# A planned decoder-step kernel: both parts of a weight tile in one buffer and one transfer, fewer transfers per inverse, and two planner margins moved

## The chip, the cores and the metric

The kernel is one program on one core of a Trainium2 chip. The metric is the device time of one execution in microseconds (us); the time before is the median of three timed runs, 1544.31 us (1543.3 to 1545.22). The engines are TensorE (PE, with its weight loads shown apart as PEld), VectorE (DVE), ScalarE (ACT), GpSimd (POOL) and SyncE (SP). In this kernel SP computes nothing: its queue issues every transfer.

## The reference

One layer of a hybrid decoder is run for a prompt of 1024 tokens and for 8 sample tokens with the same weights. Cut to what matters:

```python
p = x @ w_in                              # (T, 1024) @ (1024, 9360): GLA, RWKV-7 and gate columns
o_gla, S_gla = gla_chunked(q, k, v, log_a, S0)          # 4 heads; normed, times silu(g)
# RWKV-7, 16 heads of 64, token by token:
S = S * w[None, :] + (S @ -kk)[:, None] * (kk * a)[None, :] + v[:, None] * k[None, :]
y = S @ r                                 # then group norm, bonus, times silu(g)
m = sigmoid(gate_a) * (o_gla @ w_up_gla) + sigmoid(gate_b) * (o_rwkv @ w_up_rwkv)
out = layernorm(ALPHA * x + m @ w_out)
```

All is float32. The outputs are `out` for both groups and the new states.

## The kernel before

**Tiles and passes.** Tokens run along the free dimension in two passes: the first has 512 prompt tokens and the 8 samples, taken as 256 and 264 columns, the second has the other 512 prompt tokens in one piece. The projection goes block by block of 128 output columns (73 blocks of `w_in`, then 8 of `w_up_gla`, 8 of `w_up_rwkv`, and `w_out`). A block's weights are two half tiles of 128 x 512 (`j` = 0, 1), each with four 128 x 128 pieces.

**Three products for one.** Every float32 operand is split into a high part and a low part (`hi`, rounded; `lo = x - hi`), and a product is taken as hi·xh + hi·xl + lo·xh. `load_w` (from line 631) makes the weights' parts in the first pass: SP loads the raw half tile into `wraw`, ACT copies it to `whi`, DVE (seldom POOL) writes the difference to `wlo`. `keep` then stores both parts in DRAM, as `wh..` and `wl..`, 256 KB each. In the second pass the 146 half tiles are read back from there with two transfers each, with no work on ACT and DVE. There are four buffers `whi` and four `wlo`; `blocks` (from line 683) takes a half tile from the list `ws` and frees its two buffers after its last product.

**Pairs.** The 16 heads are done as 8 pairs in each pass, so there are 16 pairs. `front` makes the decay, key and value factors, with two sums over a head by matmul (`head_sums`, the products `big<-part,headsr`). Then come the grams: 32 products whose results DVE masks and writes to `gg` (an 'a' product and a second one, for 8 chunks and 2 heads). The 'a' products are unit triangular 64 x 64 blocks that must be inverted. Their 32 x 32 diagonal blocks go to a DRAM tile `LD` (4 transfers), from there in another arrangement to `wide` (`wide<-LD`, 4), a solve of 62 short DVE instructions fills `X` (`Xt<-X,wide` and `X<-X,Xt`), and the result goes through DRAM tile `XD` (4) to `XT` (4) and `Xs` (8); the off-diagonal blocks go to `Lp` (4). That is 28 transfers a pair. `back`, `turn`, `chain` and `norm` follow; `chain` has, for each of 8 chunks, three products in a row that wait for each other through ACT or DVE: `pch<-wide,gg`, `pch<-rh,XT`, `pch<-az,wide`.

**The samples.** The GLA state of the 8 samples is updated head by head in `gla_sample`: products `big<-row` 32 x 256, an ACT copy of 128 x 512 to a `row`, transposes `big<-cons,row`. The RWKV state of the samples (`rwkv_sample`) runs in the second pass on DVE and POOL, from eight loads `row<-state_rwkv`.

**What sets the order.** Nothing is ordered by hand. Every stage is a generator of operations, and `Order.run` (from line 368) lists them: at each step it takes the operation with the smallest modelled start time less a priority. `Order.start` models that time from when the operands are ready, with a hop between engines (`HOP`) and, for PE alone, a margin `SPARE` behind results of DVE, ACT and POOL. An operation that may run on two engines goes where it would end first. The program is that list: each engine executes its part strictly in it, and a transfer waits in SP's queue behind those ahead of it. A changed cost, margin or number of operations therefore moves rows everywhere.

Most instructions carry the line of one helper, L219, so the profile is read by the tiles' names.

Of the kernel before, what the change touches and what calls it, by code (L numbers as in the profile page):

```python
# [10 lines left out]
F32 = mybir.dt.float32  # L11
# [9 lines left out]
P = 128  # L21
D = 1024
# [4 lines left out]
HT = TP // 2  # L27
# [5 lines left out]
C = 64  # L33
NCH = HT // C
# [19 lines left out]
WBUF = {"whi": ([P, 512], 4), "wlo": ([P, 512], 4), "wraw": ([P, 512], 3)}  # L54
# [10 lines left out]
HOP = {"P": 0.2, "D": 0.8, "G": 0.14, "V": 0.14, "A": 0.14}  # L65
# [7 lines left out]
SPARE = 0.4  # L73
# [339 lines left out]
class Kern(Order):  # L413
# [217 lines left out]
    def load_w(self):  # L631

        H = NK // 2
        todo = [(b.src, b.c0, j, b.c.i) for b in self.plan if b.src is not None for j in range(2)]
        raws, his, los, kept = [], [], [], {}

        def keep(src, c0, j, hi, lo):
            for v, x in zip("hl", (hi, lo)):
                t = self.dr.tile([P, 512], F32, name=f"w{v}{c0}_{j}")
                kept.setdefault((c0, j), []).append(t)  # L640
                yield self.S.dma_start(t, x.bitcast(F32))

        def high():
            n = 0
            while True:
                yield lambda: len(raws) > n
                hi = yield from self.get("whi")
                yield self.A.copy(hi, raws[n][0])
                his.append(hi)
                n += 1  # L650
                if n == count:
                    return

        def low():
            for n in range(count):
                yield lambda: len(his) > n
                lo = yield from self.get("wlo")
                raw, src, c0, j, i = raws[n]
                yield self.E.tensor_sub(lo, raw, his[n].bitcast(F32))
                self.free(raw)  # L660
                if src is self.a["w_in"] and i == 0:
                    yield from keep(src, c0, j, his[n], lo)
                self.ws.append((his[n], lo))
                los.append(lo)
            self.w_done = True
        count = sum(src is not self.a["w_in"] or i == 0 for src, _, _, i in todo)
        self.spawn(high(), "w")
        self.spawn(low(), "w")
        for n, (src, c0, j, i) in enumerate(todo):
            if src is self.a["w_in"] and i:  # L670
                yield lambda: len(los) == len(raws)
                hi, lo = (yield from self.get("whi")), (yield from self.get("wlo"))
                for x, t in zip((hi, lo), kept[c0, j]):
                    yield self.S.dma_start(x.bitcast(F32), t)
                self.ws.append((hi, lo))
                continue
            raw = yield from self.get("wraw")
            op = self.S.dma_start(raw.rearrange("p (k c) -> p k c", c=P),
                                  src[j * H * P:(j + 1) * H * P, c0:c0 + P].rearrange("(k p) c -> p k c", p=P))
            yield from self.load(f"w{n}", op)  # L680
            raws.append((raw, src, c0, j, i))

    def blocks(self):
        xs = None
        for b in self.plan:
# [10 lines left out]
            w = []  # L696
            tiles = b.c.tiles
            todo = list(enumerate(tiles))
            while todo:
# [7 lines left out]
                for k in range(NK):  # L707
# [4 lines left out]
                    hi, lo = (x[:, k % 4 * P:k % 4 * P + P] for x in w[k // 4])  # L712
# [8 lines left out]
                    if fin and k % 4 == 3:  # L721
                        self.free(*w[k // 4])
# [378 lines left out]
    def front(self, c, p, st, d):  # L1101
# [4 lines left out]
        AZ, GG = (x.rearrange("p (c k h t) -> p c k h t", c=NCH, k=2, h=2) for x in (az, gg))  # L1106
# [72 lines left out]
        LD = self.dr.tile([4, NCH, 32, 32], F32, name=f"LD{c.i}{p}")  # L1179
# [10 lines left out]
        for q in range(4):  # L1190
            yield self.S.dma_start(L_[NU * q:NU * q + NU], LD.rearrange("n c s t -> (n c) (s t)"))
        Lp = (yield from self.get("Lp")).rearrange("p (y t) -> p y t", t=P)
        for n, b in enumerate(QS):
            h = n % 2
            yield self.S.dma_start(Lp[b, :, b], GG[QS[0], n // 2::2, 0, h, 32:64])
# [13 lines left out]
        for q in range(2):  # L1209
            b = slice(32 * q, 32 * q + 32)  # L1210
            for h in range(2):
                n = 2 * q + h
                yield self.S.dma_start(XT[HS[h]][b, :, h, b], XD[n * NCH:(n + 1) * NCH].rearrange("c s t -> s c t"))
        Xs = yield from self.get("Xs")
        xp = Xs[:, :2 * P].rearrange("p (q y t) -> p q y t", q=2, t=32)
# [311 lines left out]
    def split_out(self, raws, n):  # L1527
        for k in range(NK):
            yield lambda: len(raws) > 2 * k
            tag = "gg" if k < 2 else "wide" if k < 4 else None  # L1530
            yield lambda: k < 7 or self.w_done
            if tag == "wide":
# [7 lines left out]
            elif k < 7:  # L1540
                parts = [[x[:, :512] for x in (yield from self.get("part", 2))], (yield from self.get("lw", 2))]
            else:
                parts = [(yield from self.get("whi", 2)), (yield from self.get("wlo", 2))]
# [253 lines left out]
```

## Time and profile before

| what | value |
|---|---|
| median of 3 timed runs | 1544.31 us (1543.3 to 1545.22) |
| the profiled execution's own time | 1537.94 us |
| its span, first to last instruction | 1536.1 us |
| PE busy | 1492.0 us, 97% |
| PE weight loads busy | 1304.9 us, 85% |
| DVE, ACT, POOL busy | 1146.4, 866.7, 87.3 us |
| transfers, share of 16 engines | 70.7%, 328.60 MB |
| granted PE clock, mean | 0.995 |

The span is read in five stages: the first pass of projections (about 0 to 600 us), the second (600 to 1240), a short one in which the pairs end and the up projections begin (1240 to 1300), up and output projections (1300 to 1530), and the end. A busy PE is not a PE at its peak: the profile models the ends of its pipelined matmuls. In timeline rows the columns are start, duration, engine, line, operation, output tile and input tiles, count, and in brackets the idle time just before and what ended it.

### The profile page before, as it was taken

The page shows a single profiled execution, that of the slowest core. Times are in us where ns is not written, and L with a number is a line of the kernel's source. Part 1 is how long each engine was busy: PE and PEld are TensorE (multiplying, and loading weights), DVE is VectorE, ACT ScalarE, POOL GpSimd, SP SyncE. Part 2 cuts the span into 40 slices and gives each one's busy share as a digit, 9 for nine tenths or more (in the row PEclk, how much of TensorE's full clock was granted, in tenths as well). Part 3 has the DMA queues.
Part 4 walks back from the last instruction along what each step waited for, and adds up shares of the span by engine and source line. Part 5 has one row for each costly group of instructions (what it writes and reads, how often), then busy time and mean ns, then how long its engine had stood idle before and what let it go on. Part 6 is the DMA issues. An engine that isn't in the chain of part 4 may idle for free. (4 is left out here: it accounts for less than half of the span.)

```text
span 1536.1 us, 32633 instructions
## 1 busy us (share of the span) xinstructions
PE 1492.0 (97%) x11352; PEld 1304.9 (85%) x11352; DVE 1146.4 (75%) x3044; ACT 866.7 (56%) x2218; POOL 87.3 (6%) x202
## 2 busy tenths in 40 slices
PE   9999989999999999999999999999999999999998
PEld 8999979899999998788777778878777898988786
DVE  5785879788968896777776888888875774665665
ACT  5665576667666676564654565456346745654210
POOL 0010000001000000000001020100100000000000
PEclk9999999999999999999999999999999999999999
DMA  9878968798869887865677557656664779798522
GB/s 302 268 224 245 323 191 256 200 294 255 256 172 291 251 264 201 254 179 147 170 210 197 166 151 215 203 156 185 181 206 117 239 212 270 243 289 276 182 87 83
DMA packets 377056, 330.68 MB, mean 215 GB/s; under 512 B 131219, under 2 KB 262428, under 8 KB 376892
## 3 DMA queue, kind: packets, MB, share of 16 engines
q1 hardware_dynamic: 376892, 328.60, 70.7%
q8 instruction: 90, 1.47, 0.4%
q14 instruction: 74, 0.61, 0.1%
HBM read 198.35 MB, written 118.61 MB: 206 GB/s over the span
## 5 line engine op out<-in xcount | busy, mean ns | idle before, releaser
L219 PE MATMUL proj<-xh,whi 128*128 128x264 f32 (+2 forms) x1880 | 618.3, 329 | 5.9 <-ACT whi L219 2.7
L219 PE MATMUL proj<-xh,wlo 128*128 128x264 f32 (+2 forms) x1880 | 617.7, 329 | 0.3 <-DVE wlo L219 0.2
L219 PE MATMUL proj<-xl,whi 128*128 128x264 f32 (+2 forms) x1880 | 617.7, 329 | 0.0
L219 PEld LDWEIGHTS proj<-xh,whi 128*128 128x128 f32 x1880 | 355.6, 189 | 32.6 <-ACT row L219 3.1
L219 PEld LDWEIGHTS proj<-xh,wlo 128*128 128x128 f32 x1880 | 356.0, 189 | 24.2 <-DVE wlo L219 1.0
L219 PEld LDWEIGHTS proj<-xl,whi 128*128 128x128 f32 x1880 | 356.0, 189 | 23.4 <-issue 1.4
L219 DVE TENSOR_TENSOR wlo<-wraw,whi 128x512 fp32r<-128x512 f32 x207 | 142.2, 690 | 73.6 <-ACT whi L219 65.0
L219 ACT CAST whi<-wraw 128x512 fp32r<-128x512 f32 x210 | 129.9, 620 | 98.6 <-PE proj L219 23.1
L219 DVE TENSOR_TENSOR row<-row 128x256 f32<-128x256 f32 (+8 forms) x330 | 165.2, 509 | 20.1 <-DMA row<-state_rwkv 6.7
L219 ACT ACTIVATE row<-row 128x512 f32<-128x512 f32 (+3 forms) x229 | 138.1, 610 | 19.2 <-DVE row L219 11.2
L219 DVE TENSOR_TENSOR Xt<-X,wide 128x60 f32<-128x60 f32 (+24 forms) x496 | 105.8, 213 | 26.4 <-DMA wide<-LD 14.1
L219 DVE TENSOR_TENSOR X<-X,Xt 128x60 f32<-128x60 f32 (+24 forms) x496 | 104.7, 211 | 12.2
L219 ACT COPY rh<-pch 128x128 f32<-128x128 f32 x116 | 30.9, 267 | 131.1 <-PE pch L219 130.6
L219 ACT ACTIVATE row<-proj,omu 128x256 f32<-128x256 f32 (+1 forms) x99 | 54.1, 548 | 69.6 <-PE proj L219 68.4
L219 PE MATMUL big<-row 128*128 128x128 f32 (+4 forms) x466 | 87.0, 323 | 5.9 <-DVE row L219 4.2
L219 ACT ACTIVATE s0p<-wide,pc 64x64 f32<-64x64 f32 x256 | 89.0, 347 | 1.9
L219 POOL TENSOR_TENSOR row<-row 128x256 f32<-128x256 f32 (+7 forms) x55 | 49.5, 904 | 573.4 <-DVE row L219 313.2
L219 DVE SCALAR_TENSOR_TENSOR wide<-pch,pc,s0p 64x64 f32<-64x64 f32 x224 | 63.0, 281 | 22.8 <-PE pch L219 18.8
L219 DVE SCALAR_TENSOR_TENSOR row<-proj,pv,row 128x255 f32<-128x255 f32 (+1 forms) x99 | 56.3, 569 | 24.7 <-ACT tail L219 14.8
L219 PEld LDWEIGHTS big<-row 128*128 128x128 f32 (+3 forms) x466 | 59.0, 179 | 17.5 <-ACT row L219 6.2
L219 ACT COPY row<-big 128x128 f32<-128x128 f32 (+5 forms) x146 | 42.8, 316 | 44.9 <-PE big L219 43.9
L392 ACT ACT_TABLE_LOAD x52 | 66.7, 1283 | 0.9
(282 smaller groups left out, 2472.9 us busy)
## 6 DMA issues: line engine op xcount, KB each, us to landing
wraw<-w_in SPq DMA_DIRECT2D x146, 256.0 KB
wh<-whi SPq DMA_DIRECT2D x146, 256.0 KB
wl<-wlo SPq DMA_DIRECT2D x146, 256.0 KB
whi<-wh SPq DMA_DIRECT2D x146, 256.0 KB
wlo<-wl SPq DMA_DIRECT2D x146, 256.0 KB
wide<-LD SPq DMA_DIRECT2D x64, 128.0 KB
wraw<-w_up_gla SPq DMA_DIRECT2D x32, 256.0 KB
wraw<-w_up_rwkv SPq DMA_DIRECT2D x32, 256.0 KB
```

Source lines behind the costliest of these rows:

```text
L219: ways.append((eng, lambda call=call: call(out, *args, **kw), price(eng, name, out, args, ins)))
L392: self.nc.scalar.preload_act_table_set(self.table)
```

## The change

Three edits are made.

1. **One buffer for both parts.** `whi` and `wlo` (four of 128 x 512 each) become `wb`, four of 128 x 1024: the high part in columns 0 to 511, the low part behind it. `keep` stores a half tile with one transfer of 512 KB, rows of 4 KB, where two of 256 KB with rows of 2 KB were, and the second pass reads it back with one. `split_out` takes two `wb` for the last piece of `w_out`.
2. **The 'a' products lie together.** `gg` is laid out product by product (`k c h t`) and no longer chunk by chunk (`c k h t`), so the 16 'a' blocks of a pair are one run of 16 x 64 columns, numbered chunk by chunk with the heads inside. `LD` takes two transfers in place of four, with the same bytes; `Xs` takes four in place of eight. A pair has 22 transfers.
3. **Two margins.** `SPARE` goes from 0.4 to 0.42 and the hop from DVE from 0.14 to 0.15.

```diff
-WBUF = {"whi": ([P, 512], 4), "wlo": ([P, 512], 4), "wraw": ([P, 512], 3)}
+WBUF = {"wb": ([P, 1024], 4), "wraw": ([P, 512], 3)}
...
-HOP = {"P": 0.2, "D": 0.8, "G": 0.14, "V": 0.14, "A": 0.14}
+HOP = {"P": 0.2, "D": 0.8, "G": 0.14, "V": 0.15, "A": 0.14}
...
-SPARE = 0.4
+SPARE = 0.42
...
-        def keep(src, c0, j, hi, lo):
-            for v, x in zip("hl", (hi, lo)):
-                t = self.dr.tile([P, 512], F32, name=f"w{v}{c0}_{j}")
-                kept.setdefault((c0, j), []).append(t)
-                yield self.S.dma_start(t, x.bitcast(F32))
+        def keep(src, c0, j, x):
+            kept[c0, j] = self.dr.tile([P, 1024], F32, name=f"w{c0}_{j}")
+            yield self.S.dma_start(kept[c0, j], x.bitcast(F32))
...
-                hi = yield from self.get("whi")
-                yield self.A.copy(hi, raws[n][0])
-                his.append(hi)
+                x = yield from self.get("wb")
+                yield self.A.copy(x[:, :512], raws[n][0])
+                his.append(x)
...
-                lo = yield from self.get("wlo")
+                x = his[n]
...
-                yield self.E.tensor_sub(lo, raw, his[n].bitcast(F32))
+                yield self.E.tensor_sub(x[:, 512:], raw, x[:, :512].bitcast(F32))
...
-                hi, lo = (yield from self.get("whi")), (yield from self.get("wlo"))
-                for x, t in zip((hi, lo), kept[c0, j]):
-                    yield self.S.dma_start(x.bitcast(F32), t)
-                self.ws.append((hi, lo))
+                x = yield from self.get("wb")
+                yield self.S.dma_start(x.bitcast(F32), kept[c0, j])
+                self.ws.append(x)
...
-        AZ, GG = (x.rearrange("p (c k h t) -> p c k h t", c=NCH, k=2, h=2) for x in (az, gg))
+        AZ = az.rearrange("p (c k h t) -> p c k h t", c=NCH, k=2, h=2)
+        GG = gg.rearrange("p (k c h t) -> p c k h t", c=NCH, k=2, h=2)
+        GU = gg[:, :2 * HT].rearrange("p (u t) -> p u t", t=C)
...
-            for h in range(2):
-                yield self.S.dma_start(LD[2 * q + h].rearrange("c s t -> s c t"), GG[b, :, 0, h, b])
+            yield self.S.dma_start(LD[q].rearrange("u s t -> s u t"), GU[b, :, b])
...
-            yield self.S.dma_start(Lp[b, :, b], GG[QS[0], n // 2::2, 0, h, 32:64])
+            yield self.S.dma_start(Lp[b, :, b], GU[QS[0], n::4, 32:64])
...
-            for q in range(2):
-                u = (2 * q + n % 2) * NCH + n // 2
-                yield self.S.dma_start(xp[b, q], XD[u:(2 * q + n % 2 + 1) * NCH:2].rearrange("c s t -> s c t"))
+            yield self.S.dma_start(xp[b], XD.rearrange("(m n) s t -> n s m t", n=4)[n])
```

The list that the planner writes is new from the first rows on. PE has the same products as before; the split of copies between ACT, DVE and POOL moves by a few instructions each (DVE makes 207 of the weights' 210 low parts before and 206 now, POOL 3 and 4). SP has 1754 transfers before and 1366 now. Three places show how rows stand.

The first is PE in the first pass, at the samples of GLA head 0: the last four state products (`big<-row 32x256`) and the four transposes of their result (`big<-cons,row`), which need an ACT copy of it. Before:

```order
L219 MATMUL proj<-xl_313,whi 128x264
L219 MATMUL proj<-xh_301,wlo 128x264
L219 MATMUL big<-part,headsr 128x512
L219 MATMUL big<-row 32x256 x4
L219 MATMUL big<-cons,row 128x128 x4
L219 MATMUL proj<-xh_187,whi 128x256
```

Now, at the same head:

```order
L219 MATMUL big<-row 32x256 x4
L219 MATMUL pch<-wide,gg 128x128
L219 MATMUL proj<-xh_222,wb 128x264
L219 MATMUL proj<-xh_237,wb 128x264
L219 MATMUL proj<-xl_244,wb 128x264
L219 MATMUL proj<-xh_237,wb 128x264
L219 MATMUL proj<-xh_243,wb 128x264
L219 MATMUL proj<-xl_269,wb 128x264
L219 MATMUL proj<-xh_243,wb 128x264
L219 MATMUL big<-cons,row 128x128 x4
```

Eight products stand between the two where none stood.

The second is DVE in the second pass, at the first operation of the RWKV sample state (it reads a loaded state: `row_12160` before, `row_11648` now) and the end of a pair's `front` (up to the low half of `part`, which PE's head sum reads). The names carry buffer numbers here. Before:

```order
L219 TENSOR_TENSOR az0_167<-row_12165,row_12169 128x8x64
L219 TENSOR_TENSOR row_12161<-row_12160,row_11642 128x512
L219 SCALAR_TENSOR_TENSOR row_12167<-row_12167,row_12165 128x512
L219 TENSOR_TENSOR row_11978<-row_11978,row_12168 128x512
L219 TENSOR_TENSOR az0_167<-row_11895,row_12169 128x8x64
L219 COPY pc_12323<-row_12169 128x8
L219 COPY pc_12323<-row_12169 64x8
L219 TENSOR_TENSOR wide_12121<-row_12167,row_12166 128x8x64
L219 TENSOR_TENSOR wide_12121<-row_11978,row_12166 128x8x64
L219 SCALAR_TENSOR_TENSOR row_12168<-row_11895,pv_76,row_11978 128x512
L219 CAST part_12344<-row_12168 128x512
L219 TENSOR_TENSOR part_12345<-row_12168,part_12344 128x512
```

Now:

```order
L219 TENSOR_TENSOR wide_11546<-row_11467,row_11560 128x8x64
L219 SCALAR_TENSOR_TENSOR row_11562<-row_11340,pv_76,row_11467 128x512
L219 CAST part_11747<-row_11562 128x512
L219 TENSOR_TENSOR part_11748<-row_11562,part_11747 128x512
L219 TENSOR_TENSOR row_11643<-row_11643,row_11671 128x512
L219 TENSOR_TENSOR row_11649<-row_11648,row_11137 128x512
L219 TENSOR_TENSOR row_11467<-big_11760,row_11530 128x512
```

The state's first operation, ten rows ahead of the low half of `part` before, stands two rows behind it now.

The third is SP where the last pair's inverse ends and the up projections run: between two loads of `w_up_gla`. Before:

```order
L219 DMA wraw<-w_up_gla 128x4x128
L219 DMA mg_127<-row 128x520
L219 DMA XT_170<-XD_17660 32x8x32 x4
L219 DMA Xs<-XD_17660 32x4x32 x8
L219 DMA row<-o_rwkv 128x520
L219 DMA mg_128<-row 128x520
L219 DMA row<-o_rwkv 128x520 x7
L219 DMA az_168<-az_168 64x8x64
L219 DMA wraw<-w_up_gla 128x4x128
```

Now:

```order
L219 DMA wraw<-w_up_gla 128x4x128
L219 DMA XT_170<-XD_16831 32x8x32 x4
L219 DMA Xs<-XD_16831 32x8x32 x4
L219 DMA az_168<-az_168 64x8x64
L219 DMA row<-sg_98 128x520
L219 DMA row<-o_rwkv 128x520
L219 DMA mg_128<-row 128x520
L219 DMA row<-o_rwkv 128x520 x7
L219 DMA gg<-az_168 64x8x64 x2
L219 DMA wraw<-w_up_gla 128x4x128
```

Four `Xs` rows are gone from between the two loads, the `sg` and the two `gg` transfers have come in, and one more load of `w_up_gla` stands ahead of the group than before (15 of 16 where 14 stood).

More of the change, by code (lines that the diff above doesn't have):

```diff
@@ L656, in low @@
                 yield lambda: len(his) > n
-                lo = yield from self.get("wlo")
+                x = his[n]
                 raw, src, c0, j, i = raws[n]
-                yield self.E.tensor_sub(lo, raw, his[n].bitcast(F32))
+                yield self.E.tensor_sub(x[:, 512:], raw, x[:, :512].bitcast(F32))
                 self.free(raw)
                 if src is self.a["w_in"] and i == 0:
-                    yield from keep(src, c0, j, his[n], lo)
-                self.ws.append((his[n], lo))
-                los.append(lo)
+                    yield from keep(src, c0, j, x)
+                self.ws.append(x)
+                los.append(x)
             self.w_done = True
@@ L671, in load_w @@
                 yield lambda: len(los) == len(raws)
-                hi, lo = (yield from self.get("whi")), (yield from self.get("wlo"))
-                for x, t in zip((hi, lo), kept[c0, j]):
-                    yield self.S.dma_start(x.bitcast(F32), t)
-                self.ws.append((hi, lo))
+                x = yield from self.get("wb")
+                yield self.S.dma_start(x.bitcast(F32), kept[c0, j])
+                self.ws.append(x)
                 continue
@@ L711, in blocks @@
                         w.append(self.ws.pop(0))
-                    hi, lo = (x[:, k % 4 * P:k % 4 * P + P] for x in w[k // 4])
+                    hi, lo = (w[k // 4][:, x + k % 4 * P:x + k % 4 * P + P] for x in (0, 512))
                     xh, xl = xs[k]
@@ L721, in blocks @@
                     if fin and k % 4 == 3:
-                        self.free(*w[k // 4])
+                        self.free(w[k // 4])
                 for tt, t0, n, ps, q in qs:
@@ L1178, in front @@
         NU = 4 * NCH
-        LD = self.dr.tile([4, NCH, 32, 32], F32, name=f"LD{c.i}{p}")
+        LD = self.dr.tile([2, 2 * NCH, 32, 32], F32, name=f"LD{c.i}{p}")
         for q in range(2):
             b = slice(32 * q, 32 * q + 32)
-            for h in range(2):
-                yield self.S.dma_start(LD[2 * q + h].rearrange("c s t -> s c t"), GG[b, :, 0, h, b])
+            yield self.S.dma_start(LD[q].rearrange("u s t -> s u t"), GU[b, :, b])
         L = L_.rearrange("p (s t) -> p s t", t=32)
@@ L1211, in front @@
             for h in range(2):
[L1212 to L1213 removed]
+                yield self.S.dma_start(XT[HS[h]][b, :, h, b], XD.rearrange("(q c h) s t -> q h s c t", q=2, h=2)[q, h])
         Xs = yield from self.get("Xs")
[L1215 removed]
+        xp = Xs[:, :2 * P].rearrange("p (m t) -> p m t", t=32)
         for n, b in enumerate(QS):
[L1217 to L1219 removed]
+            yield self.S.dma_start(xp[b], XD.rearrange("(m n) s t -> n s m t", n=4)[n])
         d.AZ, d.BK, d.G, d.XT, d.v, d.bonus, d.pc, d.L = AZ, BK, GG, XT, st[2], st[1], pc, L_
@@ L1529, in split_out @@
             yield lambda: len(raws) > 2 * k
-            tag = "gg" if k < 2 else "wide" if k < 4 else None
+            tag = "gg" if k < 2 else "wide" if k < 4 else "wb" if k == 7 else None
             yield lambda: k < 7 or self.w_done
-            if tag == "wide":
+            if tag and k > 1:
                 parts = [[x[:, 0:512], x[:, 512:D]] for x in (yield from self.get(tag, 2))]
@@ L1539, in split_out @@
                 parts = [x[:2], x[2:]]
-            elif k < 7:
+            else:
                 parts = [[x[:, :512] for x in (yield from self.get("part", 2))], (yield from self.get("lw", 2))]
-            else:
-                parts = [(yield from self.get("whi", 2)), (yield from self.get("wlo", 2))]
             for hf in range(2):
```

3 lines of the change are left out of this document (1 added, 2 removed).

## The prediction

> **What bounds the kernel now.** I read the page's engine lines first, then busy time by stage, then the waits of PE, and then the timeline at PE's longest waits. The page:
>
> ```profile
> span 1536.1 us, 32633 instructions
> PE 1492.0 (97%) x11352; PEld 1304.9 (85%) x11352; DVE 1146.4 (75%) x3044; ACT 866.7 (56%) x2218; POOL 87.3 (6%) x202
> ```
>
> Busy time in the five stages, PE alone (columns: stretch, its length, PE busy with its count, granted clock, share of the DMA engines, GB/s):
>
> ```profile
> 0.00:600.00 600.00, 584.67 (x5384) 0.99 0.82 251
> 600.00:1240.00 640.00, 624.43 (x4298) 1.00 0.64 186
> 1240.00:1300.00 60.00, 54.24 (x451) 0.97 0.82 241
> 1300.00:1530.00 230.00, 228.63 (x1226) 1.00 0.61 198
> 1530.00:1536.10 6.10, 0.00 (x0) 0.77 0.25 87
> ```
>
> PE bounds every stage but the last 6 us. It idles 1536.1 - 1492.0 = 44.1 us: 15.3, 15.6, 5.8, 1.4 and 6.1 us by stage. PE's products are the same in number before and after, so the change can only win or lose idle time, and time at a lower clock. The same view of four short stretches holds much of both:
>
> ```profile
> 196.00:211.00 15.00, 9.52 (x92) 0.77 0.76 200
> 806.00:822.00 16.00, 12.50 (x107) 0.89 0.74 187
> 1245.00:1262.00 17.00, 14.48 (x106) 0.90 0.78 219
> 1270.00:1285.00 15.00, 12.12 (x99) 1.00 1.00 277
> ```
>
> Idle there: 5.48 + 3.50 + 2.52 + 2.88 = 14.4 us, a third of all in 63 us. Three of the four also show a lower clock, worth at most 0.23 x 15 + 0.11 x 16 + 0.10 x 17 = 6.9 us; where PE waits in the slow time nothing is lost, so I count 5.3 us (2.3, 1.5, 1.5).
>
> **The transfers that go.** Issue rows of SP:
>
> ```profile
> 906.04 0.32 SPq L219 DMA_DIRECT2D whi<-wh  x1
> 202.49 0.53 SPq L219 DMA_DIRECT2D wl<-wlo  x1
> 203.61 0.49 SPq L219 DMA_DIRECT2D wh<-whi  x1
> 1219.38 1.85 SPq L219 DMA_DIRECT2D LD<-gg  x4
> 1260.69 4.88 SPq L219 DMA_DIRECT2D Xs<-XD  x8
> ```
>
> Saved issue time: 146 x 0.32 us of reloads, 146 x 0.49 us of stores, 32 x 1.85/4 of `LD` and 64 x 4.88/8 of `Xs`, 47 + 72 + 15 + 39 = 173 us of SP's queue. Nearly all is hidden: the queue waits for others anyway, most of all for PE to give a weight buffer back, and PE hardly ever waits for a transfer itself.
>
> ```profile
> SPq L219 <- PE proj L219: 156.2, 103, 4.7
> PE big L219 <- DMA S<-GS: 2.0, 1, 2.0
> PE pch L219 <- DMA wide<-Sd: 1.1, 1, 1.1
> PE pch L219 <- DMA az<-wide: 1.0, 2, 0.7
> PE big L219 <- DVE Xs L219: 0.2, 1, 0.2
> ```
>
> (Columns: us in total, times, longest.) Direct waits of PE for transfers are 4.1 us and its wait for the transposed `Xs` is 0.2 us, so an inverse that ends 4 x 0.61 + 2 x 0.46 = 3.4 us earlier in each of 16 pairs gains PE 0 to 4.3 us; I take 0, since projection products cover it. Without that cover it would be up to 16 x 3.4 = 54 us.
>
> The joined reload costs nothing if it lands in time. Rows of the chain of waits:
>
> ```profile
> 1079.15 3.14 DMA whi<-wh
> 912.50 5.45 DMA wide<-LD
> 1354.10 11.10 PE pY L219 x48
> 1296.63 2.45 PE proj L219 x20
> ```
>
> A 512-wide product takes 11.10/48 = 0.231 us, a half tile 12 of them, 2.78 us. Three half tiles in hand cover 8.3 us; a transfer with 2 KB rows lands in 3.14 us, one with 4 KB rows (`wide<-LD`, 32 rows of them) in 5.45. The joined one lies between and under 8.3, so 0. If the cover were gone, the 2.3 us between the two would show at each of 146 reloads. The first pass's stores are the first rival. The grams' write to `gg` keeps 512 elements in runs of 64, so I leave its time as it is.
>
> **The four waits.** What remains is where the new list puts things. First, 203 us:
>
> ```profile
> 196.88 1.28 ACT L392 ACT_TABLE_LOAD   x1
> 202.43 0.58 ACT L219 COPY row<-big 128x512 f32<-128x512 f32 x1
> 203.07 1.12 PE L219 MATMUL big<-cons,row 128*128 128x128 f32 x4 [4.23 <-ACT row L219]
> 205.43 0.58 PE L219 MATMUL proj<-xh,whi 128*128 128x256 f32 x1 [1.24 <-ACT row L219]
> ```
>
> The transposes stand right behind the state products, and the copy that they need stands on ACT behind a table load and seven more instructions. Now eight products stand between, about 7 x 0.12 + 0.22 = 1.1 us, and ACT's list has only short chain copies and weight casts ahead of that copy. Loss now 4.23 + 1.24 + 2.3 = 7.8 us; I leave 0.5: **-7.3**.
>
> Second, 817 us:
>
> ```profile
> 791.88 5.29 SPq L219 DMA_DIRECT2D Xs<-XD  x8
> 803.97 0.48 SPq L219 DMA_DIRECT2D row<-state_rwkv  x1
> 810.44 0.69 DVE L219 TENSOR_TENSOR row<-row 128x512 f32<-128x512 f32 x1 [3.63 <-DMA row<-state_rwkv]
> 816.87 0.77 PE L219 MATMUL big<-part,headsr 128*128 128x512 f32 x1 [2.39 <-DVE part L219]
> ```
>
> DVE waits 3.63 us for the sample state, which SP issues behind the eight `Xs`, and everything that leads to `part` queues behind that; PE waits 2.39 us. Now that operation stands behind `part`, so the wait no longer reaches it: 2.39 + 1.5 of clock, **-3.9**. Late next are the operations behind it, an evacuation and the masks of the grams.
>
> Third, 1254 us:
>
> ```profile
> 1230.68 0.19 DVE L219 TENSOR_TENSOR Xt<-X,wide 128x31 f32<-128x31 f32 x1 [0.23 <-DMA wide<-LD]
> 1253.17 0.68 DVE L219 TENSOR_TENSOR part<-row,part 128x512 fp32r<-128x512 f32 x1
> 1253.91 0.80 PE L219 MATMUL big<-part,headsr 128*128 128x512 f32 x1 [2.52 <-DVE part L219]
> ```
>
> A shift on DVE, in the groups of instructions (count, busy time, mean ns of one, idle before):
>
> ```profile
> L219 DVE SCALAR_TENSOR_TENSOR row<-proj,pv,row 128x511 f32<-128x511 f32 x33 | 24.6, 745 | 7.8 <-ACT tail L219 7.3
> ```
>
> `part` stands on DVE behind the whole solve of the last pair. Between the last gram and this head sum PE's list now has 19 more products of 512, 5 more of 256 or 264 and 2 more of the chain: 19 x 0.231 + 5 x 0.12 + 2 x 0.22 = 5.4 us more. DVE's list from the last mask to `part` gains one such shift, its edge, a product and an evacuation, none of these three longer than the `part` row, and loses a small copy: at most 0.75 + 3 x 0.68 = 2.8 us. 5.4 - 2.8 = 2.6 exceeds 2.52, so the wait goes with its 1.5 us of clock: **-4.0**.
>
> Fourth, 1278 us:
>
> ```profile
> 1271.38 0.60 SPq L219 DMA_DIRECT2D wraw<-w_up_gla  x1
> 1277.45 0.62 ACT L219 CAST whi<-wraw 128x512 fp32r<-128x512 f32 x1 [13.01 <-DMA wraw<-w_up_gla]
> 1278.12 0.38 PE L219 MATMUL proj<-xh,whi 128*128 128x256 f32 x1 [2.65 <-ACT whi L219]
> ```
>
> PE ran out of weights because a load queued behind `XT`, `Xs` and eight `row<-o_rwkv`. Four issues leave (2.4 us) and one more half tile is loaded ahead, but three other transfers enter, and the DMA engines were full (share 1.00). Of 2.88 us I take half: **-1.4** (0 to -2.9).
>
> **What the list adds.** At two places `pch<-az,wide` now follows `pch<-rh,XT` with only one projection product between, about 0.23 us, where at least 0.79 us stood before. Each costs from 0 to the largest wait of such a product above, 1.1 us: **+2.0**. New long waits that I cannot see: from 0 to as much as the four that go (14.4 + 5.3 = 19.7 us), since the same planner made them. I take a quarter, nearer to 0 because the covers of head sums and chain products that I compared are otherwise alike: **+5**. The other 44.1 - 14.4 - 6.1 = 23.6 us of idle time I leave.
>
> Sum: -7.3 - 3.9 - 4.0 - 1.4 + 2.0 + 5 = **-9.6 us**. The profiled execution's own time is 1537.94 us, 1.84 above its span, and would become 1528.3. The median of the timed runs is 1544.31, 6.4 above the profiled one, so I predict **1534.7 us**.
>
> The clock terms come from the rows: waits of 2.39 and 2.52 us were each followed by a stretch at less than the full clock. The Trainium skill, "TensorE: Matmul & The Clock Gate", section "Why this matters for your kernels", asks for no idle gaps of PE over about 3 us. By that rule only the first wait would cost clock, and the sum would be 3.0 us smaller, -6.6, still within the forecast's range. The trace decides here, and it differs from the rule: shorter waits sufficed.
>
> **Rivals.**
>
> *The waits come back elsewhere* (no change). For it: all rows moved, and the four long waits are what this planner's margins let through once already. Against it: each of the four had a cause that I could find, and PE's covers did not shrink in general. With 16.6 us regained and as much lost anew: 1544 (1539 to 1549).
>
> *The stores with 4 KB rows fill the DMA engines* (slower). The place is the first pass. Its DMA share is 0.82 at 251 GB/s over 600 us, 150.6 MB, of which the stores are 146 x 0.524 = 76.5 MB, so 0.42 of share. From 43% more time per stored byte the share is 1 and the weight loads behind them set the pace; each further 10% is 0.042 x 600 = 25 us. At 50% more: 17 us, so 1534.7 + 17 = 1552. For it: `wide<-LD`, the only row with 4 KB rows, lands 128 KB in 5.45 us, where 256 KB take 3.14. Against it: it writes only 32 partitions, the stores read 128.
>
> *Nothing new goes wrong* (the whole gain). The four waits go and no long one comes: -17, 1527.
>
> That the change does not do what it says is out: the list has 32 `LD`, 64 `Xs` and 292 weight transfers where 64, 128 and 584 were.
>
> **How the numbers follow.** The forecast gets 0.54 (its own range 1527 to 1540), the waits elsewhere 0.27, the whole gain 0.11, the stores 0.08. A measurement of this kernel tells about 0.2% from no change, 3.1 us: faster is under 1541.2, slower over 1547.4. Faster: 0.54 + 0.11 + 0.05 of the second case = 0.70; same 0.15, all of the second case; slower 0.07 of the second case + 0.08 = 0.15. The range: -19 us (all waits gone, the fourth whole, 1525) to +4 (the second case's upper part, 1548); the far ends of the second case and the stores are left out.
>
> **What would show it.** In the changed profile: PE idle of some 38 us in place of 44; no wait above 2 us at the transposes of the first GLA head, nor at a head sum in front of the sample states, nor at the last pair's; full clock in the first 600 us. PE's direct waits for transfers stay near 4 us. Wrong would be: a DMA share near 1 in the first 600 us; waits of ACT for weight buffers that a store still holds; new PE waits over 2.4 us with a lower clock behind them, or waits over 1 us at `pch<-az,wide` in many chunks.

## The result and the profile after

The changed kernel takes **1535.8 us** (median of 5 runs, 1531.6 to 1537.2), the kernel before 1543.75 in the same comparison (median of 5, 1540.6 to 1545.2): ratio 0.9944, 95% interval 0.9923 to 0.9964. The forecast was 1534.7. The time came out near the forecast; the experiments below show that the sum behind it did not.

The profiled execution of the changed kernel took 1536.23 us, close to its median. That of the kernel before took 1537.94, some 6 below its own, so the two profiles differ less than the medians do. Span and PE line of the page, then PE by stage (columns as in the prediction):

```profile
span 1534.5 us, 31929 instructions
PE 1493.6 (97%) x11352; PEld 1305.9 (85%) x11352; DVE 1150.6 (75%) x3065; ACT 865.8 (56%) x2210; POOL 84.2 (5%) x189
```

```profile
0.00:600.00 600.00, 585.80 (x5433) 1.00 0.80 250
600.00:1240.00 640.00, 622.04 (x4215) 0.99 0.64 186
1240.00:1300.00 60.00, 59.11 (x506) 1.00 0.88 260
1300.00:1530.00 230.00, 226.62 (x1205) 1.00 0.61 199
```

PE idles 1534.5 - 1493.6 = 40.9 us, 3.2 less than before. Its busy time is 1.6 us more with the same 11352 products: that is time at a lower clock. The third stage gained most (54.24 to 59.11 of 60), the second pass lost (624.43 to 622.04 of 640). The same view of the four stretches of the prediction, and of three where the changed kernel loses:

```profile
196.00:211.00 15.00, 14.79 (x187) 1.00 0.87 256
806.00:822.00 16.00, 16.00 (x132) 1.00 0.62 172
1245.00:1262.00 17.00, 16.53 (x134) 1.00 0.85 265
1270.00:1285.00 15.00, 15.00 (x147) 1.00 1.07 318
845.00:862.00 17.00, 14.81 (x121) 0.90 0.49 112
1012.00:1030.00 18.00, 16.16 (x158) 0.81 0.52 143
1165.00:1182.00 17.00, 14.58 (x96) 0.80 0.58 148
```

In the first four PE is busy 62.3 of 63 us, where it was 48.6, all at the full clock. In the other three it idles 2.19 + 1.84 + 2.42 = 6.45 us, and the clock takes up to 0.10 x 17 + 0.19 x 18 + 0.20 x 17 = 8.5 us. The last of the three is not wholly new: before, PE waited 2.0 us for the same load at that head, but at the full clock. The waits of PE (us in total, times, longest):

```profile
PE big L219 <- DVE row L219: 6.3, 6, 2.0
PE big L219 <- DMA S<-GS: 4.3, 2, 2.4
PE pch L219 <- DVE az L219: 1.2, 2, 0.7
PE pch L219 <- DMA az<-wide: 1.0, 1, 1.0
```

`S<-GS` is the load of a GLA head's state, stored by the first pass; the second pass needs it once for each of four heads. It holds two of the three new stretches; the larger sum, for `row`, is spread over six waits.

### The profile page after: what moved, and what is told of

Its sections match the earlier page's. It is cut to its first block, busy times and chain, and to the rows that moved or that the text cites. A ratio compares the mean times of both kernels' runs of the same rounds, so it can differ in the third digit from the quotient of the medians.

```text
span 1534.5 us, 31929 instructions
## 1 busy us (share of the span) xinstructions
PE 1493.6 (97%) x11352; PEld 1305.9 (85%) x11352; DVE 1150.6 (75%) x3065; ACT 865.8 (56%) x2210; POOL 84.2 (5%) x189
## 5 line engine op out<-in xcount | busy, mean ns | idle before, releaser
L219 PE MATMUL proj<-xh,wb 128*128 128x256 f32 (+2 forms) x3744 | 915.6, 327 | 2.1 <-DVE wb L219 0.9
L219 PEld LDWEIGHTS proj<-xh,wb 128*128 128x128 f32 x3744 | 627.0, 189 | 49.0 <-issue 2.5
L219 PE MATMUL proj<-xl,wb 128*128 128x264 f32 (+2 forms) x1872 | 613.2, 328 | 0.0
L219 PEld LDWEIGHTS proj<-xl,wb 128*128 128x128 f32 x1872 | 354.4, 189 | 23.5 <-issue 2.1
L219 DVE TENSOR_TENSOR wb<-wraw,wb 128x512 fp32r<-128x512 f32 x206 | 141.6, 691 | 55.3 <-ACT wb L219 52.2
L219 DVE TENSOR_TENSOR row<-row 128x512 f32<-128x512 f32 (+9 forms) x342 | 167.3, 495 | 14.1 <-ACT row L219 4.9
L219 ACT CAST wb<-wraw 128x512 fp32r<-128x512 f32 x210 | 129.8, 620 | 78.4 <-PE proj L219 31.6
L219 ACT ACTIVATE row<-row 128x512 f32<-128x512 f32 (+4 forms) x229 | 138.2, 611 | 31.7 <-DVE row L219 19.8
L219 PE MATMUL big<-xh,wb 128*128 128x512 f32 (+2 forms) x272 | 70.8, 332 | 0.0
L219 PE MATMUL pY<-xh,wb 128*128 128x264 f32 (+2 forms) x256 | 63.5, 319 | 0.0
```

The lines of the kernel that those rows point to most:

```text
L219: ways.append((eng, lambda call=call: call(out, *args, **kw), price(eng, name, out, args, ins)))
```

## The experiments

Each median is over 4 to 12 runs, taken in turns with runs of the kernel before, whose median was 1542.8 to 1543.4 us in all four sets (the changed kernel's are those above, beside 1543.75). "Transfers" is how many SP issues by the trace (1752 and 1364, two fewer than were counted in the two lists); idle is span less PE's busy time of the profiled execution. That execution is one run only: it was the slowest of its kernel's runs in the tenth to the twelfth, and the fastest in the seventh.

| kernel | list of the engines | transfers on SP | median us (range) | ratio to before, interval | PE idle | PE busy |
|---|---|---|---|---|---|---|
| before | its own | 1752 | 1543 | 1 | 44.1 | 1492.0 |
| changed | its own | 1364 | 1535.8 (1531.6 to 1537.2) | 0.9944, 0.9923 to 0.9964 | 40.9 | 1493.6 |
| 1 all in two | changed | 1752 | 1562.5 (1561.2 to 1565.4) | 1.0129, 1.0114 to 1.0145 | 59.5 | 1501.0 |
| 2 margins only | new | 1752 | 1566.9 (1565.4 to 1569.5) | 1.0157, 1.0142 to 1.0173 | 60.0 | 1505.7 |
| 3 old margins | new | 1364 | 1558.4 (1558.0 to 1561.1) | 1.0104, 1.0089 to 1.0119 | 59.6 | 1496.6 |
| 4 state early | changed | 1364 | 1526.0 (1524.2 to 1526.3) | 0.9886, 0.9870 to 0.9903 | 38.8 | 1485.4 |
| 5 inverse in two | changed | 1460 | 1557.5 (1555.0 to 1558.7) | 1.0094, 1.0075 to 1.0114 | 54.7 | 1502.0 |
| 6 weights in two | changed | 1656 | 1539.6 (1532.2 to 1548.8) | 0.9986, 0.9966 to 1.0006 | 41.0 | 1494.2 |
| 7 all in two, state early | changed | 1752 | 1548.5 (1543.1 to 1552.6) | 1.0036, 1.0023 to 1.0049 | 48.5 | 1492.7 |
| 8 22 a pair | before | 1656 | 1531.0 (1529.9 to 1531.7) | 0.9924, 0.9906 to 0.9942 | 38.4 | 1489.7 |
| 9 gathers in two | changed | 1428 | 1552.6 (1549.9 to 1554.6) | 1.0065, 1.0045 to 1.0084 | 51.3 | 1500.1 |
| 10 second halves by POOL | changed | 1364 | 1538.8 (1533.6 to 1541.4) | 0.9969, 0.9952 to 0.9986 | 47.1 | 1492.5 |
| 11 state early, XT by POOL | changed | 1300 | 1522.75 (1521.8 to 1528.8) | 0.9878, 0.9857 to 0.9900 | 37.7 | 1489.3 |
| 12 as 11 | before | 1592 | 1527.0 (1526.6 to 1530.9) | 0.9895, 0.9873 to 0.9916 | 36.7 | 1492.4 |

A list is kept by leaving what the planner sees unchanged and replacing only what it emits at a place (`ways` holds what an operation issues). PE's products then stand in the same order in both kernels, and the difference of their ends, product by product, shows where time is lost.

### 1. The same list with all its transfers back

The prediction put the saved transfers at nothing. The plainest test is to give them back and leave all else.

```diff
-            yield self.S.dma_start(kept[c0, j], x.bitcast(F32))
+            op = self.S.dma_start(kept[c0, j], x.bitcast(F32))
+            t = kept[c0, j]
+            fn = lambda: [self.nc.sync.dma_start(t[:, s], x.bitcast(F32)[:, s]) for s in (slice(0, 512), slice(512, 1024))]
+            op.ways = [(op.ways[0][0], fn, op.ways[0][2])]
+            yield op
```

The reload, `LD` and `Xs` are split in the same way.

> The changed kernel's list on TensorE, VectorE, ScalarE and GpSimd, instruction for instruction, but every joined transfer (store and reload of the split weights, the inverse's read of the 32-wide blocks, the gather of its rows) is issued as two again: SyncE issues 1752 transfers as the kernel before does, not 1364. Theory A (the saved transfers are hidden; the time goes by the waits of TensorE that the list happens to hold): 1536 us, within 3, as the changed kernel's 1535.8. Theory B (the gain is the saved transfers): 1543.8, as before. Theory C (the two margins do it): 1536.

It takes 1562.5 us, 26.7 more than the changed kernel: theory A has fallen. PE by pass, and its waits for the load:

```profile
0.00:600.00 600.00, 583.77 (x5403) 1.00 0.81 248
600.00:1240.00 640.00, 607.16 (x4061) 0.98 0.61 179
```

```profile
PE big L219 <- DMA S<-GS: 12.9, 3, 5.7
```

Most is lost in the second pass. In the profiled executions the 26.3 us grow by 4.8 up to 640 us, then by some 4 at 870, 4.9 at 978, 4.4 at 1020, 3.3 at 1172 and 3.2 between 1250 and 1265 us of the changed kernel. At 870, 1020 and 1172 the wait is for `S<-GS`. SP's timeline ahead of the last of them, the changed kernel first, then this one:

```profile
1156.79 3.21 SPq L219 DMA_DIRECT2D XD<-X  x4
...
1161.56 1.82 SPq L219 DMA_DIRECT2D XT<-XD  x4
1163.42 2.12 SPq L219 DMA_DIRECT2D Xs<-XD  x4
1165.59 0.64 SPq L219 DMA_DIRECT2D az<-az  x1
1166.33 0.57 SPq L219 DMA_DIRECT2D wb<-w  x1
1166.94 0.43 SPq L219 DMA_DIRECT2D S<-GS  x1
```

```profile
1176.51 3.44 SPq L219 DMA_DIRECT2D XD<-X  x4
...
1181.98 2.15 SPq L219 DMA_DIRECT2D XT<-XD  x4
1184.17 3.77 SPq L1226 DMA_DIRECT2D Xs<-XD  x8
1187.99 0.65 SPq L219 DMA_DIRECT2D az<-az  x1
1189.05 0.83 SPq L676 DMA_DIRECT2D wb<-w  x2
1189.92 0.43 SPq L219 DMA_DIRECT2D S<-GS  x1
```

SP has no pause here. It issues one transfer after the other, about half a microsecond each (3.77 us for eight, 2.12 for four), and the state's load stands at the end of the line: 10.15 us behind the first `XD` in the one, 13.41 in the other. PE's products behind that load, in the same two kernels (in brackets the wait):

```profile
1171.84 0.79 PE L219 MATMUL big<-row,S 128*128 128x128 f32 x2 [2.42 <-DMA S<-GS]
```

```profile
1194.87 0.80 PE L219 MATMUL big<-row,S 128*128 128x128 f32 x2 [5.72 <-DMA S<-GS]
```

3.26 us later in the line, 3.30 us more of waiting. This is theory D of the later experiments: what counts is how long SP issues ahead of a load that PE, or work for PE, waits for.

### 2 and 3. The margins alone, and the rest alone

```diff
-HOP = {"P": 0.2, "D": 0.8, "G": 0.14, "V": 0.14, "A": 0.14}
+HOP = {"P": 0.2, "D": 0.8, "G": 0.14, "V": 0.15, "A": 0.14}
...
-SPARE = 0.4
+SPARE = 0.42
```

The second kernel is the one before with this edit; the third is the changed kernel with its opposite.

> The kernel before with the two margins alone (0.42 and 0.15); all transfers as before. Theory A: a new list with new waits, so anywhere from 1528 to 1548 us; the difference to 1543.8 should be found again as PE's idle time and as stretches at a clock of 0.5. Theory B: 1543.8, no difference. Theory C: 1535.8, the whole gain.

> The changed kernel's joined weights and 22 transfers a pair, with the old margins (0.4 and 0.14). Theory A: again a list of its own, 1528 to 1548 us, with idle time and stretches at 0.5 that account for it. Theory B: 1535.8, the whole gain. Theory C: 1543.8, none of it.

1566.9 and 1558.4 us: both outside every theory's range. Each part of the change alone makes the kernel slower, by 24 and 15 us. The same two margins, which change nothing but what the planner lists in which order and on which engine, cost 24 us in the kernel before and gain 23 (1558.4 to 1535.8) with the rest of the change. PE in the first pass and the longest single wait of the second kernel, then the same of the third:

```profile
0.00:600.00 600.00, 576.12 (x5240) 0.98 0.81 246
```

```profile
PE proj L219 <- ACT whi L219: 5.3, 2, 4.5
```

```profile
0.00:600.00 600.00, 576.97 (x5289) 0.99 0.80 250
```

```profile
PE big L219 <- DVE Xs L219: 4.2, 2, 3.6
```

Both lose some 8 us in a first pass that was busy 584.67 us before; besides, the one runs out of weights for 4.5 us at 1305 us, and the other waits 3.6 for an inverse's rows at 593 us, where the kernel before waited 0.2 for such rows in all. So a new list is worth some 24 us either way, several times the +5 that the prediction took for unseen waits and more than its bound of 19.7, and the time of a part alone tells nothing of that part.

### 4. The state's load at the start of the head

The load is issued where the head begins, 35 to 42 us before its use; the planner still believes it at the old place.

```diff
+        S0 = None
+        if c.i:
+            S0 = self.take("S")
+            self.nc.sync.dma_start(S0, self.GS[h])
...
-            S = yield from self.get("S")
-            yield S_.dma_start(S, self.GS[h])
+            S = S0
+            op = S_.dma_start(S, self.GS[h])
+            op.ways = [(op.ways[0][0], lambda: None, op.ways[0][2])]
+            yield op
```

> The changed kernel with one thing moved: the load of a GLA head's stored state in the second pass is issued at the start of the head and not just ahead of its use; every other instruction keeps its place on its engine. In the changed kernel TensorE waits 2.0 us at 1020 and 2.9 us at 1172 for that load, and the clock is at 0.5 for 6.83 us behind each. If these waits cost what the trace shows (about 2.4 us each of idle time and up to 3.4 us each by the clock), the time falls by 4.5 (the waits alone) to 11 us (with the clock), to 1525 to 1531 us, most likely 1527. If something else is as late there (VectorE's rows, the next bank), it falls by less than 2 us.

1526.0 us, 9.8 less than the changed kernel and 1.0 off the expectation. The last head's load, then PE in the three bad stretches (each shifted by the time gained):

```profile
1126.91 0.42 SPq L787 DMA_DIRECT2D S<-GS  x1
```

```profile
845.00:862.00 17.00, 14.81 (x129) 1.00 0.50 122
1008.00:1026.00 18.00, 17.89 (x186) 1.00 0.64 166
1154.00:1172.00 18.00, 17.62 (x134) 1.00 0.67 174
```

The two waits are gone, and the clock is full. Product by product, PE gains 5.0 us at the one place and 5.6 at the other. PE's waits there were 1.84 and 2.42 us (not the 2.0 and 2.9 of the expectation), so more than half of what each cost was clock. The smaller steps elsewhere nearly cancel: of the 10.3 us between the spans, 2.1 are idle time and 8.2 are PE's busy time, for the same products. The first stretch, which lies ahead of that head's use of the load (868 us), idles as long as in the changed kernel (2.19 us) and yet keeps the clock, so that gain, about 1.5 us, is not shown to be the load's.

### 5, 6 and 9. Which transfers

> The changed kernel's list, with the inverse's transfers alone issued in two (28 a pair, 1460 in all); the weights stay joined. Theory A has fallen by the first run (1562.5 us where it gave 1536). Theory D in its place: in the second pass SyncE issues its transfers in one line, and the load of the stored GLA state, for which TensorE waits, stands behind the inverse's gathers and one to four reloads of weights; twice the gathers keep it back by 1.65 to 2.3 us (3.77 against 2.12, 5.09 against 2.75 us), the reloads by 0.3 to 0.5 each. D gives the inverse's 96 transfers some half of the 26.6 us: 1549 us, from 1544 to 1556. Theory E (each of the 388 transfers costs alike, 0.069 us): 96 x 0.069 = 6.6, so 1542.4.

> The changed kernel's list, with the weights' stores and reloads alone issued in two (1656 transfers); the inverse has 22 a pair. Theory D: 1546 us, from 1540 to 1553 (what stands ahead of the state's load grows by 0.3 to 1.5 us, and the stretch at 989 us, where three reloads take 8.99 for 4.10 us, is theirs). Theory E: 292 x 0.069 = 20.1, so 1556.

The inverse's 96 transfers cost 21.7 us, more than theory D's range allowed, the weights' 292 cost 3.8, just under its range; the sixth kernel's interval overlaps the changed kernel's, and its 12 runs spread over 16.6 us. (The 8.99 against 4.10 us in its expectation sets three reloads beside two.) Theory E, the same price for each transfer, had 6.6 and 20.1 and falls. What matters is where a transfer stands. Of the 96, 64 are the gathers into `Xs`:

> The changed kernel's list, with only the gather of the inverse's rows into Xs issued in two (64 transfers more, 1428 in all); the read of the blocks and the weights stay joined. The fifth run put 21.7 of the 26.6 us on the inverse's 96. Theory D (what counts is how long SyncE issues ahead of transfers that TensorE or the inverse waits for): the gathers are the part that stands ahead of the state's load, so two thirds or more of 21.7: 1551 us, from 1546 to 1558. Theory E (alike for each): 64 / 96 x 21.7 = 14.5, so 1550. If the read of the blocks, which begins the inverse, counts most: 1543 or less.

1552.6 us, 16.8 more than the changed kernel for these 64. That the reading of the blocks counts most would have given 1543 or less and is out; that each of the 96 costs alike gives 1550, which this run does not tell from theory D.

### 10. The same transfers, half of the gathers issued by POOL

If SP's issue time is what counts, the second halves should cost nothing when another engine issues them.

```diff
-            yield self.S.dma_start(xp[b], XD.rearrange("(m n) s t -> n s m t", n=4)[n])
+            op = self.S.dma_start(xp[b], XD.rearrange("(m n) s t -> n s m t", n=4)[n])
+            fn = lambda n=n, b=b: [e.dma_start(xp[b, m], XD.rearrange("(m n) s t -> n s m t", n=4)[n][:, m])
+                                   for m, e in ((slice(0, 4), self.nc.sync), (slice(4, 8), self.nc.gpsimd))]
+            op.ways = [(op.ways[0][0], fn, op.ways[0][2])]
+            yield op
```

> As the ninth, with each second half of those gathers issued by GpSimd's queue, so that SyncE issues 1364 transfers as in the changed kernel, while the same 1428 transfers run. Theory D (SyncE's issue time is what counts): back to the changed kernel's 1536 us, within 4. Theory G (smaller transfers land later or fill the DMA engines): as the ninth run, 1546 to 1558. If GpSimd's issue is slow (no row shows one), between the two, with TensorE waiting for Xs.

1538.8 us: 13.8 of the 16.8 are back, with the same 1428 transfers. The other 3.0 are within the runs' ranges; in its profile, a slow one, PE still waits 6.5 us for the state's load (8.5 in the ninth, 4.3 in the changed kernel). Timelines at the third head, SP of the ninth kernel, then SP of the tenth and its POOL:

```profile
1019.24 5.11 SPq L1214 DMA_DIRECT2D Xs<-XD  x8
1024.39 0.66 SPq L219 DMA_DIRECT2D az<-az  x1
```

```profile
1009.73 2.81 SPq L1214 DMA_DIRECT2D Xs<-XD  x4
1012.58 1.51 SPq L219 DMA_DIRECT2D az<-az  x1
```

```profile
1008.09 1.66 POOL L1214 DMA_DIRECT2D Xs<-XD  x3 [5.78 <-PE big L219]
```

Theory G, that smaller transfers land later or fill the DMA engines, would have left it where the ninth is. Theory D stands: it is SP's time to issue them. The Trainium skill, "DMA: Bandwidth & Descriptors", section "Rules for kernel authors", says that spreading transfers over issuing engines adds no bandwidth and saves only the sequencer's issue time; the run agrees with the saving, which was the 13.8 us here, and tests nothing of the bandwidth.

### 7. All transfers in two, the state's load early

> The first experiment's kernel (the changed list, all transfers in two, 1752) with the state's load moved to the start of the head, as in the fourth. Theory D, if the state's load is the one transfer that matters: its three waits (12.9 us) go, and with them most of what the clock took (PE's busy time is 7.4 us above that of the changed kernel): 1562.5 - 20 = 1542 us, and between 1536 and 1546. If the saved transfers count at many places, it stays at 1550 or above.

1548.5 us, 14 below the first kernel but 22.5 above the fourth: between the two cases of the expectation. So the state's load is not the only one that the line holds back, and, of what the split costs, not the main part: with that load out of the way the split transfers still cost 22.5 us, against 26.7 with it in its old place. Product by product against the fourth kernel (17.3 us between the two profiles, as the seventh's was its fastest run) it loses 7.7 us up to 640 us in steps of 1 to 2 us, and 4.5 at once at 987 us, where a load of an RWKV state is late:

```profile
PE pch L219 <- DMA wide<-Sd: 4.6, 2, 3.6
```

### 8. The old list with 22 transfers a pair

The changed layout of `gg` and the joined reading and gathering, in the kernel before with its own list; the weights stay in two, the margins are the old ones. The planner still counts 28: it sees both halves, the first issues the whole and the second nothing.

```diff
-            yield self.S.dma_start(xp[b], XD.rearrange("(m n) s t -> n s m t", n=4)[n])
+            for m in (slice(0, 4), slice(4, 8)):
+                op = self.S.dma_start(xp[b, m], XD.rearrange("(m n) s t -> n s m t", n=4)[n][:, m])
+                fn = (lambda: None) if m.start else lambda n=n, b=b: self.nc.sync.dma_start(
+                    xp[b], XD.rearrange("(m n) s t -> n s m t", n=4)[n])
+                op.ways = [(op.ways[0][0], fn, op.ways[0][2])]
+                yield op
```

> The kernel before with its own list on TensorE, VectorE, ScalarE and GpSimd, and only the inverse's transfers joined (22 a pair, 1656 in all), which its planner did not know of. Theory D: that list holds one wait for the state's load (2.0 us at 1170, behind 6.80 us from issue to use), so 1 to 4 us are to be had: 1541 us, from 1538 to 1544. Theory E: 96 x 0.069 = 6.6, so 1536.7. Theory A: 1543.

1531.0 us, 11.8 less than before and 4.9 less than the changed kernel: more than any theory gave. SP at the last head, the kernel before and then this one:

```profile
1156.45 3.78 SPq L219 DMA_DIRECT2D Xs<-XD  x8
...
1165.88 0.45 SPq L219 DMA_DIRECT2D S<-GS  x1
```

```profile
1151.40 1.92 SPq L1223 DMA_DIRECT2D Xs<-XD  x4
...
1160.22 0.42 SPq L219 DMA_DIRECT2D S<-GS  x1
```

PE of this kernel in the prediction's first three stretches (the third shifted by 7 us) and at that head:

```profile
196.00:211.00 15.00, 9.52 (x86) 0.66 0.74 194
806.00:822.00 16.00, 13.99 (x111) 0.89 0.47 139
1160.00:1182.00 22.00, 21.61 (x207) 1.00 0.35 85
1238.00:1256.00 18.00, 15.33 (x111) 0.91 0.78 225
```

At the head PE was busy 19.62 of the same 22 us before. The first and the third long wait are still there (4.23 and 2.67 us), as they must be if the list makes them; the second is shorter (12.50 busy before), because the sample state behind the gathers comes sooner (DVE waits 1.68 us for it, 3.63 before). The fourth, for weights whose load stood behind the gathers, falls from 2.65 to 0.73 us, with no change of the list.

### 11 and 12. SP's line made shorter still

The four gathers into `XT` go to POOL's queue, on top of the state's early load; first in the changed kernel, then in the eighth.

```diff
-                yield self.S.dma_start(XT[HS[h]][b, :, h, b], XD.rearrange("(q c h) s t -> q h s c t", q=2, h=2)[q, h])
+                op = self.S.dma_start(XT[HS[h]][b, :, h, b], XD.rearrange("(q c h) s t -> q h s c t", q=2, h=2)[q, h])
+                fn = lambda q=q, h=h, b=b: self.nc.gpsimd.dma_start(
+                    XT[HS[h]][b, :, h, b], XD.rearrange("(q c h) s t -> q h s c t", q=2, h=2)[q, h])
+                op.ways = [(op.ways[0][0], fn, op.ways[0][2])]
+                yield op
```

> The fourth kernel (state's load at the start of the head, 1526 us) with the four gathers into XT, which stand ahead of the four into Xs and take SyncE 1.8 to 2.2 us a pair, issued by GpSimd's queue. Theory D: Xs and all behind it come 2 us earlier in 16 pairs; what PE still waits for there (0.9 us for Xs, 1.1 us for a state of the other layer) is small with 22 transfers, so 0 to 4 us: 1523 us, from 1520 to 1526. If GpSimd issues much slower than SyncE, XT is late at the products that follow and the time rises to 1530 to 1540.

> The eighth kernel (the list of before, weights in two, 22 transfers a pair, 1531 us) with the two moves of the eleventh: the state's load at the start of the head, the gathers into XT on GpSimd's queue. If the lists are worth the same once SyncE's line is short, it comes to the eleventh's 1523 us, within 3. If the list of before has nothing that waits behind SyncE any more (its trace shows no wait for the state's load), it stays at 1531, from 1528 to 1533, and the new list with its joined weights is the better one by 8.

1522.75 and 1527.0 us. The eleventh is the fastest kernel here, 13 us below the changed one, and as expected; its interval overlaps the fourth's, so the step from 1526.0 to 1522.75 is not told from nothing. The twelfth lies between the two cases of its expectation. The two differ by 4.3 us, within the runs' ranges; and since the twelfth also has its weights in two, which cost 3.8 in the sixth, this says nothing of the lists.

## Why the prediction was right, and where it was not

**The time was right by luck: two wrong terms cancelled.** The prediction had -9.6: nothing for the transfers (but for a part of the fourth wait), the rest for the list. The runs have a gain from the transfers and a loss from the list, by either road: the old list with 22 transfers a pair is 11.8 us faster, and the rest of the change then costs 4.9; or the new list with all transfers costs 19 us, and joining them gains 26.7. Each list was made for its own number of transfers, so neither road gives the one true share of each. Nor can the terms be settled one by one: they were read from the profiled execution, and between the two profiled executions the change is 1.6 us, where the forecast had 9.6; only the medians differ by 7.95.

**"Nearly all is hidden"** is the step that failed. It took SP's 173 us as hidden since SP mostly waits for PE, and bounded the gain of the inverse by PE's direct waits for transfers, 4.1 us in all (4.4 with `row<-OS`, which it left out). The runs give 26.7 us for all 388 transfers and 21.7 for the inverse's 96. Both averages look away from the place that matters. SP waits long on the whole, but not between an inverse's first `XD` and what follows it: there the issue time is the path (10.15 against 13.41 us). And the direct waits are those of a list that was made with 28 transfers; they don't bound what stands just inside its cover, nor what goes through another engine. The prediction's own rows for 817 us show such a case, DVE waiting 3.63 us for a sample state issued behind eight `Xs`; I read it as a matter of DVE's order alone.

**The joined weights, 0,** are not contradicted: taking them apart costs 3.8 us, with overlapping intervals. PE's wait for the state's load is no longer with them apart than joined (3.9 us in the sixth kernel's profile, 4.3 in the changed one's).

**The four waits, -16.6,** were right at their places: 13.7 us of idle time gone, the fourth wait whole where I took half, and the first 600 us at the full clock. But they are not all the list's. By the eighth kernel the shorter line of SP alone takes most of the fourth wait and part of the second. The third went by a cover that the prediction put only 0.1 us above the wait, and it needs the joined transfers too: at this head sum PE waits 0.47 us in the changed kernel, 2.32 with the weights in two, 2.12 with all in two and 3.59 with the inverse in two (0.48 with the gathers alone in two), all with the changed list. Only the first wait is shown to be the list's alone.

**The two new places at `pch<-az,wide`, +2.0,** show as 1.2 us in two waits of `pch` for `az` (0.52 and 0.70, at just these places): within 0 to 2.2, a little over half of the value.

**New long waits, +5 (0 to 19.7),** is the mis-sized term. The three new stretches alone hold 6.45 us of idle time and up to 8.5 of clock, near 15 (13 without the 2.0 us that stood there before), within the range and far from the value. And this is the changed kernel, with fewer transfers; the first kernel's second pass is busy 607.16 us where the kernel before had 624.43.

**The clock** was counted behind waits of 2.39 and 2.52 us; in the changed kernel 1.84 and 2.42 us sufficed, as the windows at 1012 and 1165 us show. The rule that I weighed, no idle gaps over about 3 us (the Trainium skill, "TensorE: Matmul & The Clock Gate", "Why this matters for your kernels"), again speaks of longer gaps than these; the measurement decides.

**The rivals.** The stores that fill the DMA engines did not come: the share in the first pass is 0.80 after 0.82. "The waits come back elsewhere" was nearly right on the list and missed what pays for it. Of the signs named beforehand, PE's idle time (40.9, forecast 38) and its direct waits for transfers (4.3 + 1.0, forecast near 4) came close. The sign that did fire was a new wait of over 2.4 us with a lower clock behind it.

**What stays open.** Why the lists of the second and third kernel are so much worse was not taken apart, nor where the rest of the seventh's 22.5 us arises beyond the steps named. That the eighth kernel gains 11.8 us by medians and 8.0 between the profiled executions is because the profile of before is a fast one. Its mean clock is 0.995, while the timed runs of before have 0.990 to 0.995, so some of the missing 3.8 us may be clock; no trace here shows it.

## What to carry to other kernels

Before a transfer is called hidden, look at what stands behind it in the same queue, and whether the queue pauses in between: in a burst without a pause each issue delays all that follows, whatever the queue's share of idle time. Where a planner makes the order, test a change with the order held fixed, in the old list and in the new one; the order redrawn by two margins alone moved this kernel by 24 us, more than the change it carried. A load that is needed long after its input is ready belongs at the head of the burst, not behind it: one moved line was worth more than the whole change.

## What the runs showed of the hardware

SP's line issues one of these transfers in about half a microsecond, and POOL's queue a gather of the same kind in a similar time (three in 1.66 us), beside its other work. Neither was expected to set PE's pace, and SP's did.

The clock's price follows no simple length of wait. PE at the fifth kernel's third head, behind its longest wait (5.9 us by its list of waits), and the fourth kernel at a place with 2.89 us of idle time:

```profile
1031.00:1046.00 15.00, 12.60 (x110) 0.54 0.25 66
```

```profile
974.00:986.00 12.00, 9.11 (x44) 1.00 0.80 216
```

The first ran about 13.7 of the 15 us at half the clock, the second none. Two single waits of almost one length, the first in the changed kernel with 6.83 us at half the clock behind it, the second in the fourth kernel with none:

```profile
1019.90 0.49 PE L219 MATMUL big<-row,S 128*128 128x128 f32 x2 [1.84 <-DMA S<-GS]
```

```profile
975.83 0.49 PE L219 MATMUL pch<-rh,XT 128*128 128x128 f32 x2 [1.97 <-DVE rh L219]
```

In the stretch at 845 us the same 2.19 us of idle time cost clock in the changed kernel (0.90) and none in the fourth (1.00), with the same list. The Trainium skill ("TensorE: Matmul & The Clock Gate", "What's actually happening") describes a window of about 3.4 us that runs freely and isn't set off by the kernel; a wait would then cost clock or not by where it falls in it.

The clock records of the traces agree, and show more. From where they begin (5 to 11 us after the start) up to the end of PE's work, every stretch at half the clock lasts 3.41, 6.83, 10.24 or 13.65 us, and within one trace the stretches begin whole multiples of 3.41 us apart (in the changed kernel at 853.93, 1021.18 and 1171.37 us, 49 and 44 multiples). Cut into such windows, all fourteen traces together give this for a window at the full clock: with over 1.85 us of idle time of PE in it the next ran at half the clock (37 of 37), between 1.64 and 1.85 us it did in 8 of 15, below that it did once (1.16 us) in over 6000. The 1.84 us above lie in one window, the 1.97 are divided between two, 0.65 and 1.32. So two waits close together can cost as much as a longer one: the changed kernel's at 845 us are 1.36 and 0.82 us, in one window. The grid also lies differently in each trace, which may be why runs of one kernel differ as they do; no run here tests that.
